# Decoding the expert choices one token block at a time, and preparing the last four expert slots first, in a decoder block on one core

## The chip, the cores and the metric

The kernel runs on one core of a Trainium2 chip. The metric is the device time of one execution in microseconds (us). The engines are named as in the profile: PE (TensorE: matrix products, with PEld its weight loads), DVE (VectorE), ACT (ScalarE), POOL (GpSimd) and SP (the queue that issues most of the DMAs). [...]

## The reference

One decoder block over 512 tokens of width 1024: an attention sub-layer (a sliding-window group and a stick-breaking group), a layer norm, then a sub-layer in which every token picks experts out of 16,384, and a second layer norm. The expert part, which the change touches, is this:

```python
q  = einsum('bsd,dk->bsk', xm, w_q).reshape(b, s, 8, 2, 128)
sc = einsum('bshpc,hpnc->bshpn', q, sub_keys)            # 8 heads, 2 halves, 128 keys
top_s, top_i = top_k(sc, 16)
cand = top_s[..., 0, :, None] + top_s[..., 1, None, :]   # 16 x 16 pairs
best_s, best_c = top_k(cand, 16)
i1 = take_along_axis(top_i[..., 0, :], best_c // 16)     # which key of half 0
i2 = take_along_axis(top_i[..., 1, :], best_c % 16)      # which key of half 1
expert = i1 * 128 + i2
g = softmax(best_s)
y[token] = sum over its 128 experts of g * gelu(xm . u[expert]) * v[expert]
```

All in float32 at the interfaces; the kernel holds most matrix operands as a high and a low part.

## The kernel before

**The expert part as matrix products.** The tokens are four blocks of 128. For blocks 1 to 3 (384 tokens) the kernel doesn't gather: it goes through all 128 slots of 128 experts. A U slot is 24 matmuls of 384 columns into `ph` (three for each of 8 chunks: `uhi` with `h2hi`, `uhi` with `h2lo`, `ulo` with `h2hi`), then Gelu into `stash`; a V slot is 18 matmuls of 512 columns into `yb`, with the weighted stash (`ghi`, `glo`) against the slot's rows of v (`vhi`, `vlo`). The weights are a table W of 384 tokens by 16,384 experts, built on chip from one-hot rows (`pw`) and written to `w_d`. Block 0 gathers its own experts' rows on POOL's DMA queue, and DVE works on them.

**High and low parts.** `split` (L91) makes `hi` with a copy on ACT and `lo` with a subtraction of 128x1024 on DVE or, where `eng=G`, on POOL. Two buffers each for `uhi` and `ulo`, so that the next slot's `uhi` starts when the slot two before it is done on PE. The third matmul of a slot needs `ulo`.

**The gate stage.** While DVE picks the top 16 (`top16`, L618 to L622, `cand` L632), PE runs U slots as cover. The last four of these (`MIDDLE`, recorded at L137) come directly before the choices are decoded, with their low parts on POOL. The last of them is called slot M here, and the one after it, the first of `u_steps`, slot N; N's `ulo` is made on DVE (the `split` in `cut`). From there on the order of instructions is the order of the code, on each engine. `decode` turns the 16 positions of every token and head into key positions `sel`, and the scores into weights `gall` (subtract, Exp on ACT, sum, reciprocal, multiply), on all four blocks at once (512 columns). `level2` of a block looks up `i1` and `i2` with one-hot compares of 128x2048 (`oh` L715, times `tabx` L717, folded L721), transposes (`ptr` L737) and makes the rows `tr` (L744, L745). Block 1's `level2` comes before the loop, interleaved with quarters of U slots (6 matmuls each) on PE.

**The W loop.** 96 groups of four tokens: `build` and `scale` (L758, L766, 128x1024) on DVE three groups ahead, 8 matmuls `pw` and about one quarter of a U slot on PE, and a share of the `level2` of the next block on DVE.

**The last stretch.** U slots run 32 ahead of V slots (`LOOK`), so the last V slots stand alone. `prep` makes a slot's operands: `gt` (L920), `glo` (L956), the v row's low part (L958); `heads` makes the high parts on ACT. `ghi` has three buffers and `glo` two; the last six slots (`GROUP`) take `glast` from the freed stash ring, and the last four put their v rows into the space of `h2hi` and `h2lo`, which U slots used before. `vraw` has three buffers, loaded by SP. The last six slots run as a group for each block and half of the columns, so that each token block is finished (`finish`: gate, add, layer norm, out) while PE works for the next.

## Time and profile before

| what | value |
|---|---|
| time, median of 3 runs | 1597.37 us (1597.34 to 1597.96) |
| the profiled execution: time, span | 1595.99 us, 1594.3 us |
| mean granted clock of PE in it | 0.985 |
| PE, DVE, ACT, POOL busy | 98%, 77%, 41%, 29% |
| PE's share of the chain that ended last | 79% |

The span is from the first to the last instruction; 1.7 us of the execution's time lie outside it. A busy PE is one with a matmul under way, at whatever clock.

### The profile page before, as it was taken

What the parts mean: (1) busy time and instruction counts of PE and PEld (TensorE: products, weight loads), DVE (VectorE), ACT (ScalarE), POOL (GpSimd) and SP (SyncE); (2) the same over time, 40 slices, a digit from 0 to 9 for tenths busy, and PEclk for the clock granted to TensorE, in tenths of its full rate; (3) what the DMA queues carried; (4) which work ended last, traced back from release to release, by engine and by line L of the source; (5) the groups of instructions that cost most, each with busy time, mean ns of one, the idle gap of its engine ahead of it and who ended that gap; (6) DMA issues with size and microseconds to landing.
All of it is one profiled execution on the core that took longest, in us unless ns stands there. A gap on an engine that the chain in (4) does not pass through costs nothing.

```text
span 1594.3 us, 21985 instructions
## 1 busy us (share of the span) xinstructions
PE 1554.9 (98%) x8109; PEld 1346.3 (84%) x8109; DVE 1220.3 (77%) x2351; ACT 647.5 (41%) x935; POOL 455.8 (29%) x410
## 2 busy tenths in 40 slices
PE   8999999999989999999999999999999999999996
PEld 5776767788879999899999999999999999998885
DVE  2568585589999997578777787777877777777878
ACT  2535574333355555333333333333333333333331
POOL 0002133544400000233334333333333444333100
PEclk8999898999999999999999999999999999999999
DMA  9564132222225555999888988999889998989873
GB/s 338 184 258 158 53 112 101 79 92 81 81 80 212 219 210 202 334 327 326 305 311 301 326 301 304 306 309 322 302 303 312 307 321 301 311 282 305 261 231 119
DMA packets 147356, 382.12 MB, mean 240 GB/s; under 512 B 11312, under 2 KB 68656, under 8 KB 143280
## 3 DMA queue, kind: packets, MB, share of 16 engines
q1 hardware_dynamic: 110384, 246.49, 44.6%
q0 software_dynamic: 36864, 134.23, 24.4%
q8 instruction: 63, 1.03, 0.3%
q14 instruction: 45, 0.37, 0.1%
HBM read 351.32 MB, written 29.36 MB: 239 GB/s over the span
## 4 chain that ended last, share of the span: by engine, by line
PE 79%; DVE 12%; DMA 3%; ACT 3%; issue 1%; POOL 1%; SPq 0%; DVEq 0%; ACTq 0%; POOLq 0%
PE yb L980 32%; PE ph L970 25%; PE pw L841 5%; PE ph L806 4%; PE pj L303 3%; PE zm L556 2%; DVE scr L620 1%; PE pj L274 1%; DMA wa<-in_wada_dram 1%; DVE tsi L622 1%; DVE tsi L619 1%; PE pq L647 1%; DVE tsv L621 1%; DVE tsv L618 1%; PE oacc L398 1%
## 5 line engine op out<-in xcount | busy, mean ns | idle before, releaser
L855 POOL DMA_INDIRECT gat<-in_u_rows_dram,idx x128 | 161.6, 1262 | 478.5 <-DVE hd L873 226.5
L93 DVE TENSOR_TENSOR ulo<-uraw,uhi 128x1024 fp32r<-128x1024 f32 x133 | 162.5, 1223 | 164.9 <-ACT uhi L92 160.5
L970 PE MATMUL ph<-h2hi,ulo 128*128 128x384 f32 x768 | 258.6, 337 | 0.6 <-DVE ulo L93 0.6
L970 PE MATMUL ph<-h2hi,uhi 128*128 128x384 f32 x768 | 258.2, 336 | 0.3 <-ACT uhi L92 0.3
L970 PE MATMUL ph<-h2lo,uhi 128*128 128x384 f32 x768 | 258.2, 336 | 0.0
L855 POOL DMA_INDIRECT gat<-in_v_rows_dram,idx x128 | 161.0, 1258 | 264.8 <-DVE y L883 224.1
L980 PE MATMUL yb<-vhi,ghi 128*128 128x512 f32 x654 | 203.0, 391 | 0.0
L980 PE MATMUL yb<-vhi,glo 128*128 128x512 f32 x654 | 202.9, 391 | 0.0
L980 PE MATMUL yb<-vlo,ghi 128*128 128x512 f32 x654 | 202.6, 391 | 0.0
L92 ACT ACTIVATE uhi<-uraw 128x1024 fp32r<-128x1024 f32 x155 | 162.4, 1050 | 74.6 <-PE pq L647 52.9
L883 DVE SCALAR_TENSOR_TENSOR y<-gat,cf,y 128x1024 f32<-128x1024 f32 x127 | 162.7, 1281 | 3.9 <-DMA gat<-in_v_rows_dram,idx 1.6
L873 DVE CUSTOM_DVE_ANT_0 gscr<-gat,h2row 128x1024 f32<-128x1024 f32 x128 | 156.5, 1222 | 10.6 <-DMA gat<-in_u_rows_dram,idx 7.9
L1085 ACT ACTIVATE stash<-ph 128x384 f32<-128x384 f32 x96 | 47.2, 491 | 275.1 <-PE ph L970 275.1
L970 PEld LDWEIGHTS ph<-h2lo,uhi 128*128 128x128 f32 x768 | 144.4, 188 | 4.4
L970 PEld LDWEIGHTS ph<-h2hi,uhi 128*128 128x128 f32 x768 | 144.4, 188 | 4.4 <-ACT uhi L92 0.7
L980 PEld LDWEIGHTS yb<-vlo,ghi 128*128 128x128 f32 x654 | 122.7, 188 | 27.3
L980 PEld LDWEIGHTS yb<-vhi,glo 128*128 128x128 f32 x654 | 122.8, 188 | 26.8
L970 PEld LDWEIGHTS ph<-h2hi,ulo 128*128 128x128 f32 x768 | 144.4, 188 | 1.0 <-DVE ulo L93 1.0
L980 PEld LDWEIGHTS yb<-vhi,ghi 128*128 128x128 f32 x654 | 121.8, 188 | 18.9
L93 DVE TENSOR_TENSOR vlo<-vraw,vhi 128x1024 fp32r<-128x1024 f32 x97 | 118.4, 1220 | 17.5 <-ACT vhi L92 17.4
L92 ACT ACTIVATE vhi<-vraw 128x1024 fp32r<-128x1024 f32 x97 | 102.8, 1060 | 53.6 <-issue 35.8
L947 ACT ACTIVATE ghi<-gt 128x384 fp32r<-128x384 f32 x97 | 51.0, 525 | 177.7 <-DVE gt L920 177.7
(311 smaller groups left out, 2860.1 us busy)
## 6 DMA issues: line engine op xcount, KB each, us to landing
uraw<-in_uT_dram SPq DMA_DIRECT2D x128, 512.0 KB, 5.2
vraw<-in_v_rows_dram SPq DMA_DIRECT2D x128, 512.0 KB, 5.2
w_d<-stage SPq DMA_DIRECT2D x12, 2048.0 KB, 7.3
wt<-w_d SPq DMA_DIRECT2D x32, 768.0 KB, 9.3
wa<-in_wada_dram SPq DMA_DIRECT2D x16, 1024.0 KB, 6.5
wah<-in_wada_dram SPq DMA_DIRECT2D x16, 512.0 KB, 9.4
uraw<-in_wq_dram SPq DMA_DIRECT2D x16, 512.0 KB, 3.3
uraw<-in_wqk_dram SPq DMA_DIRECT2D x11, 512.0 KB, 7.8
```

Source lines behind the costliest of these rows:

```text
L92: A.activation(hi, src, AF.Copy)
L93: (eng or V).tensor_tensor(lo, src, hi.bitcast(F32), op=OP.subtract)
L303: T.matmul(p, a[:, dc], b[:, dc], start=(dc == 0 and n == 0), stop=(dc == DC - 1 and n == 2))
L806: T.matmul(p[:, :ND], a[:, dc], b[:, dc, P:], start=(dc == 0 and n == 0), stop=(dc == DC - 1 and n == 2))
L841: T.matmul(p[:, k * P:(k + 1) * P], oh4[:, 1, :, k], oh4[:, 2 + j, :, k], start=(j == 0), stop=(j == 1), skip_group_check=True)
L855: G.indirect_dma_start(out=t, out_offset=None, in_=rows, in_offset=bass.IndirectOffsetOnAxis(ap=idx[:, k:k + 1], axis=0))
L873: V.tensor_tensor_reduce(out=scr, in0=t, in1=h2row, scale=1.0, scalar=0.0, op0=OP.mult, op1=OP.add, accum_out=hd[:, n:n + 1])
L883: V.scalar_tensor_tensor(y0, t, cf[:, k:k + 1], y0, op0=OP.mult, op1=OP.add)
L947: A.activation(gop[i][0], gts[i], AF.Copy)
L970: T.matmul(p[:, :ND], a[:, dc], b[:, dc, P:], start=(dc == 0 and n == 0), stop=(dc == DC - 1 and n == 2))
L980: T.matmul(ybank[b][c0 // 512][:, c0 % 512:(c1 - 1) % 512 + 1], x[:, t], y[:, c0:c1], start=(i == 0 and n == 0), stop=(n == 2 and i == (NK ...
L1085: A.activation(stash[i + LOOK], p[:, :ND], AF.Gelu_apprx_tanh)
```

## The change

In the gate stage the decoding is cut by token block. `weights` now comes first: the subtraction and the Exp for all four blocks, and the copy of the key indices. `decode(t0, t1)` then does block 1 alone (128 columns); blocks 2 and 3 (256 columns) and block 0 (128 columns) are decoded inside the W loop, ahead of the `level2` that needs them, at 19 steps a block where there were 15. Fewer steps stand before the loop, so that 12 quarters of U slots come before its first `pw` where there were 15, and three more inside it. Slot M's low part goes from POOL to DVE, and slot N's from DVE to POOL.

In the last stretch the last 14 slots (`OWN`) take `glast` for their weighted stash, where the last six did. The order of slots is now `seq`: 0 to 121, then 124 to 127, then 122 and 123. From slot 114 on operands are prepared four slots ahead and more, where it was two. `finish` of block 0 takes two steps a slot.

```diff
 GROUP = 6
+OWN = 14
 PRE = 0
...
 
-    def decode():
-        n = TB * P
-        pos = flat(bsp)
-        tmp = mw.tile([P, 4, n], BF16, name="dec", tag="oh", bufs=1)
+    def weights():
+        V.tensor_tensor(gall, bsv, bsv[:, :, :, 0:1].to_broadcast([P, TB, NH, TOPK]), op=OP.subtract)
+        A.activation(gall, gall, AF.Exp)
+        A.activation(tib, tsi, AF.Copy)
+
+    def decode(t0, t1):
+        c = slice(t0 * P, t1 * P)
+        pos = flat(bsp)[:, c]
+        tmp = mw.tile([P, 4, TB * P], BF16, name="dec", tag="oh", bufs=1)[:, :, c]
         pf, m1, m2, mk = (tmp[:, k] for k in range(4))
         d = pf
-        mi = mw.tile([P, n], U32, name="mi", tag="tabx", bufs=1)
-        A.activation(tib, tsi, AF.Copy)
+        mi = mw.tile([P, TB * P], U32, name="mi", tag="tabx", bufs=1)[:, c]
+        s0, s1 = sel[:, 0, c], sel[:, 1, c]
         V.tensor_copy(pf, pos)
-        yield
         V.tensor_scalar(m1, pf, 16.0, None, op0=OP.is_ge)
...
         V.tensor_tensor(mi, pos, mi, op=OP.bitwise_and)
-        yield
-        V.tensor_copy(sel[:, 1], mi)
-        V.tensor_tensor(d, pf, sel[:, 1], op=OP.subtract)
+        V.tensor_copy(s1, mi)
+        V.tensor_tensor(d, pf, s1, op=OP.subtract)
         yield
...
         V.tensor_tensor(d, d, mk, op=OP.mult)
-        yield
         V.tensor_tensor(d, d, m1, op=OP.subtract)
-        V.scalar_tensor_tensor(sel[:, 0], m2, -63.0, d, op0=OP.mult, op1=OP.add)
-        yield
-        V.tensor_tensor(gall, bsv, bsv[:, :, :, 0:1].to_broadcast([P, TB, NH, TOPK]), op=OP.subtract)
-        A.activation(gall, gall, AF.Exp)
+        V.scalar_tensor_tensor(s0, m2, -63.0, d, op0=OP.mult, op1=OP.add)
         yield
-        V.tensor_reduce(gsum[:, :, :, 0], gall, axis=AX.X, op=OP.add)
-        V.reciprocal(gsum, gsum)
-        V.tensor_tensor(gall, gall, gsum.to_broadcast([P, TB, NH, TOPK]), op=OP.mult)
+        g, q = gall[:, t0:t1], gsum[:, t0:t1]
+        V.tensor_reduce(q[:, :, :, 0], g, axis=AX.X, op=OP.add)
+        V.reciprocal(q, q)
+        V.tensor_tensor(g, g, q.to_broadcast([P, t1 - t0, NH, TOPK]), op=OP.mult)
         yield
...
 
-        def cut(s):
+        def cut(s, eng=V):
             if s < n1:
                 hl[s] = [wsp.tile([P, DC, P], F32R, name=f"u{e}", tag=f"u{e}") for e in ("hi", "lo")]
-                split(raws.pop(s), *hl[s])
+                split(raws.pop(s), *hl[s], eng)
 
...
         load(n0 + 1)
-        cut(n0)
+        cut(n0, G)
         yield
...
 
-    def slot_now():
-        u_slot(len(stash), bank("h", "ph", bufs=2), ring.tile([P, ND], F32, name="stash"))
-
-    for _ in range(MIDDLE):
-        slot_now()
+    for n in range(MIDDLE):
+        u_slot(len(stash), bank("h", "ph", bufs=2), ring.tile([P, ND], F32, name="stash"),
+               V if n == MIDDLE - 1 else G)
     man = tc.manual_schedule()
...
     next(us)
-    for n, _ in enumerate(chain(decode(), level2(1))):
+    weights()
+    for n, _ in enumerate(chain(decode(1, 2), level2(1))):
         if 2 * n >= 3 * done:
...
         if i % per == 0:
-            lv, ln = level2((2 + i // per) % TB), 0
+            tb = (2 + i // per) % TB
+            todo = () if tb == 3 else decode(tb, 4 if tb == 2 else 1)
+            lv, ln = chain(todo, level2(tb)), 0
         build(i + AHEAD)
...
         evac(i - 1)
-        while ln < 15 * (i % per + 1) / (per - AHEAD - 1):
+        while ln < 19 * (i % per + 1) / (per - AHEAD - 1):
             next(lv, None)
...
     vseen = set()
+    seq = list(range(NK - GROUP)) + list(range(NK - 4, NK)) + list(range(NK - GROUP, NK - 4))
 
-    def load_v(i):
-        if i < NK and i not in vseen:
+    def load_v(n):
+        i = seq[min(n, NK - 1)]
+        if n < NK and i not in vseen:
             vseen.add(i)
...
     def load_w(c):
-        if c < NK // WR:
+        if c < NK // WR and c not in wts:
             w = mw.tile([P, NTG, WR, TG], F32, name="wt")
...
         gts[i] = g.rearrange("p a t -> p (a t)")
-        gop[i] = [mw.tile([P, ND], F32R, name=f"g{e}", tag=f"g{e}", bufs=k) for e, k in (("hi", 3), ("lo", 2))]             if i < NK - GROUP else [
+        gop[i] = [mw.tile([P, ND], F32R, name=f"g{e}", tag=f"g{e}", bufs=k) for e, k in (("hi", 3), ("lo", 2))]             if i < NK - OWN else [
             ring.tile([P, ND], F32R, name="glast", tag="stash") for _ in range(2)]
...
 
-    def prep(i, units):
+    def prep(n, units):
         units = list(units)
+        i = seq[n] if n < NK else n
         alone = i + LOOK > NK
         if alone:
-            heads(i)
-            heads(i + 1)
+            for k in (n, n + 1):
+                if k < NK:
+                    load_w(seq[k] // WR)
+                    heads(seq[k])
         elif i < NK:
...
                 split(vraw.pop(i), *vop[i])
-        fetch_to(i + (LEAD if i + LOOK >= NK else 1))
+        fetch_to(n + (LEAD if n + LOOK >= NK else 1))
         for n in units:
...
                          start=(i == 0 and n == 0),
-                         stop=(n == 2 and i == (NK - GROUP - 1 if b == TB - 2 else NK - 1)) or c1 - c0 < 512,
+                         stop=(n == 2 and i == (NK - GROUP - 1 if b == TB - 2 else seq[-1])) or c1 - c0 < 512,
                          skip_group_check=(c1 - c0 < 512))
...
             return i + 1
-        return min(i + 2, NK - GROUP - 1) if i < NK - GROUP - 3 else min(NK, 2 * i - (NK - GROUP) + 8)
+        if i < NK - OWN:
+            return i + 2
+        return min(i + 4 + 3 * max(0, i - (NK - GROUP - 5)), NK)
 
...
             next(f0, None)
+            next(f0, None)
         if i == NK - GROUP - 1:
...
         for c in pieces(b + 1):
-            for i in range(NK - GROUP, NK):
+            for i in seq[NK - GROUP:]:
                 v_mm(i, b, (c,))
```

Three places in the order of DVE's instructions follow. The first is the end of the last head's `best`, where the decoding starts; `scr`, `bsv` and `bsp` are of the top 16, `ulo` is a U slot's low part. Before:

```order
L620 MATCH_REPLACE scr_3699<-bsv,cand 128x80
L621 MAX bsv<-scr_3699 128x8
L622 MAX_INDEX bsp<-bsv,scr_3699 128x8
L93 TENSOR_TENSOR ulo<-uraw,uhi 128x1024
L680 CAST dec<-bsp 128x512
L682 TENSOR_SCALAR dec<-dec 128x512
L683 TENSOR_SCALAR dec<-dec 128x512
L684 TENSOR_SCALAR dec<-dec 128x512
L686 SCALAR_TENSOR_TENSOR mi<-dec 128x512
```

After:

```order
L621 MATCH_REPLACE scr_3699<-bsv,cand 128x80
L94 TENSOR_TENSOR ulo<-uraw,uhi 128x1024
L622 MAX bsv<-scr_3699 128x8
L623 MAX_INDEX bsp<-bsv,scr_3699 128x8
L674 TENSOR_TENSOR gall<-bsv 128x512
L686 CAST dec<-bsp 128x128
L687 TENSOR_SCALAR dec<-dec 128x128
L688 TENSOR_SCALAR dec<-dec 128x128
L689 TENSOR_SCALAR dec<-dec 128x128
L691 SCALAR_TENSOR_TENSOR mi<-dec 128x128
```

The `ulo` ahead of the last MAX is slot M's; before, M's was POOL's, and the `ulo` that stood behind the last MAX_INDEX was slot N's. The subtraction of `gall` now stands ahead of the decoding, which is 128 wide.

The second place is the start of the W loop, where `oh_N` numbered rows are the one-hot rows for successive groups (L758 build, L766 scale). Before:

```order
L758 TENSOR_TENSOR oh_4025<-iota_2417,tr 128x1024
L758 TENSOR_TENSOR oh_4027<-iota_2417,tr 128x1024
L766 TENSOR_TENSOR oh_4025<-oh_4025,tr 128x1024
L758 TENSOR_TENSOR oh_4030<-iota_2417,tr 128x1024
L766 TENSOR_TENSOR oh_4027<-oh_4027,tr 128x1024
L758 TENSOR_TENSOR oh_4033<-iota_2417,tr 128x1024
L766 TENSOR_TENSOR oh_4030<-oh_4030,tr 128x1024
L715 TENSOR_TENSOR oh<-iota_2415,sel 128x2048
L758 TENSOR_TENSOR oh_4057<-iota_2417,tr 128x1024
L766 TENSOR_TENSOR oh_4033<-oh_4033,tr 128x1024
```

After:

```order
L759 TENSOR_TENSOR oh_4003<-iota_2417,tr 128x1024
L767 TENSOR_TENSOR oh_4000<-oh_4000,tr 128x1024
L759 TENSOR_TENSOR oh_4006<-iota_2417,tr 128x1024
L767 TENSOR_TENSOR oh_4003<-oh_4003,tr 128x1024
L686 CAST dec<-bsp 128x256
L687 TENSOR_SCALAR dec<-dec 128x256
L688 TENSOR_SCALAR dec<-dec 128x256
L689 TENSOR_SCALAR dec<-dec 128x256
L759 TENSOR_TENSOR oh_4033<-iota_2417,tr 128x1024
L767 TENSOR_TENSOR oh_4006<-oh_4006,tr 128x1024
L94 TENSOR_TENSOR ulo<-uraw,uhi 128x1024
L691 SCALAR_TENSOR_TENSOR mi<-dec 128x256
```

A quarter of the decoding of blocks 2 and 3 stands between two builds, where before it was the first compare of the next block's lookup, and the next part follows behind the `ulo`.

The third place is the last operands on DVE; `h2lo` is the low part of the v row of slots 124 to 127, `vlo` and `ulo` that of others. Before:

```order
L958 TENSOR_TENSOR h2lo<-vraw,h2hi 128x1024
L1038 SCALAR_TENSOR_TENSOR y_2423<-y_2423,l2rs,ln_13770 128x512 x2
L920 TENSOR_TENSOR gt<-stash,wt 128x384
L956 TENSOR_TENSOR glast<-gt,glast 128x384
L958 TENSOR_TENSOR h2lo<-vraw,h2hi 128x1024
L920 TENSOR_TENSOR gt<-stash,wt 128x384
L956 TENSOR_TENSOR glast<-gt,glast 128x384
L958 TENSOR_TENSOR h2lo<-vraw,h2hi 128x1024
L956 TENSOR_TENSOR glast<-gt,glast 128x384
L958 TENSOR_TENSOR h2lo<-vraw,h2hi 128x1024
```

After:

```order
L965 TENSOR_TENSOR h2lo<-vraw,h2hi 128x1024
L924 TENSOR_TENSOR gt<-stash,wt 128x384
L963 TENSOR_TENSOR glast<-gt,glast 128x384
L965 TENSOR_TENSOR h2lo<-vraw,h2hi 128x1024
L924 TENSOR_TENSOR gt<-stash,wt 128x384
L963 TENSOR_TENSOR glast<-gt,glast 128x384
L965 TENSOR_TENSOR h2lo<-vraw,h2hi 128x1024
L924 TENSOR_TENSOR gt<-stash,wt 128x384
L963 TENSOR_TENSOR glast<-gt,glast 128x384
L965 TENSOR_TENSOR vlo<-vraw,vhi 128x1024
L963 TENSOR_TENSOR glast<-gt,glast 128x384
L965 TENSOR_TENSOR ulo<-vraw,uhi 128x1024
```

The operands in the space of `h2lo` now come ahead of two that go to ordinary buffers (slots 122 and 123), and the last part of block 0's `finish` (L1038) is no longer between them.

## Rows read from the trace of the kernel before

**Rows 1.** The page: the span, two engines, and the lines of the chain
```profile
span 1594.3 us, 21985 instructions
...
PE 1554.9 (98%) x8109; PEld 1346.3 (84%) x8109; DVE 1220.3 (77%) x2351; ACT 647.5 (41%) x935; POOL 455.8 (29%) x410
...
PE yb L980 32%; PE ph L970 25%; PE pw L841 5%; PE ph L806 4%; PE pj L303 3%; PE zm L556 2%; DVE scr L620 1%; PE pj L274 1%; DMA wa<-in_wada_dram 1%; DVE tsi L622 1%; DVE tsi L619 1%; PE pq L647 1%; DVE tsv L621 1%; DVE tsv L618 1%; PE oacc L398 1%
```

**Rows 2.** Windows: busy us by engine, granted clock (PEclk), DMA share, GB/s
```profile
437.80:461.00 23.20, 18.52 (x88) 17.40 (x87) 20.27 (x34) 12.46 (x15) 0.00 (x0) 0.85 0.28 91
...
452.00:454.00 2.00, 2.00 (x8) 2.00 (x7) 1.86 (x5) 1.97 (x2) 0.00 (x0) 0.50 0.64 234
...
480.00:500.00 20.00, 20.00 (x145) 18.29 (x144) 20.00 (x33) 10.70 (x16) 0.00 (x0) 1.00 0.64 232
...
655.00:1443.00 788.00, 788.00 (x3993) 717.07 (x3992) 608.82 (x749) 286.48 (x382) 305.87 (x241) 1.00 0.90 311
```

**Rows 3.** Timeline of PE, 427 to 475 us
```profile
432.50 0.34 PE L137 MATMUL ph<-h2hi,ulo 128*128 128x384 f32 x1
...
445.41 0.34 PE L806 MATMUL ph<-h2hi,ulo 128*128 128x384 f32 x1
...
449.60 0.69 PE L806 MATMUL ph<-h2hi,uhi 128*128 128x384 f32 x1 [3.85 <-ACT uhi L92]
...
456.14 0.44 PE L806 MATMUL ph<-h2hi,uhi 128*128 128x384 f32 x1
...
462.67 1.11 PE L841 MATMUL pw<-oh 128*128 128x128 f16 x8 [0.95 <-DVE oh L766]
...
472.10 1.11 PE L841 MATMUL pw<-oh 128*128 128x128 f16 x8 [0.27 <-DVE oh L766]
```

**Rows 4.** Timeline of DVE, 428 to 463 us
```profile
429.16 2.48 DVE L632 TENSOR_TENSOR cand<-tsv 128x16 f32<-128x16 f32 x2
...
435.45 0.23 DVE L620 MATCH_REPLACE8 scr<-bsv,cand 128x80 f32<-128x80 f32 x1
...
436.22 1.21 DVE L93 TENSOR_TENSOR ulo<-uraw,uhi 128x1024 fp32r<-128x1024 f32 x1
...
437.35 0.42 DVE L680 CAST dec<-bsp 128x512 bf16<-128x512 uint32 x1
...
445.03 0.69 DVE L701 TENSOR_REDUCE gsum<-gall 128x32 f32<-128x512 f32 x1 [0.70 <-ACT gall L699]
...
446.75 1.22 DVE L715 TENSOR_TENSOR oh<-iota,sel 128x2048 bf16<-128x2048 bf16 x1
...
449.57 1.23 DVE L93 TENSOR_TENSOR ulo<-uraw,uhi 128x1024 fp32r<-128x1024 f32 x1 [1.61 <-ACT uhi L92]
...
460.52 0.29 DVE L745 TENSOR_TENSOR tr<-gr,tr 128x128 f16<-128x128 f32 x1
...
461.93 0.68 DVE L766 TENSOR_TENSOR oh<-oh,tr 128x1024 f16<-128x1024 f16 x1
```

**Rows 5.** Line L632 by engine: least, median and longest in ns
```profile
L632 DVE TENSOR_TENSOR cand<-tsv x7: 156/178/2403, 428.8 to 432.1; 128x32 f32<-128x32 f32 x2, 128x20 f32<-128x20 f32 x1, 128x16 f32<-128x16 f32 x1, 128x12 f32<-128x12 f32 x1
```

**Rows 6.** Timelines of POOL and ACT, 427 to 449 us
```profile
429.21 2.40 POOL L93 TENSOR_TENSOR ulo<-uraw,uhi 128x1024 fp32r<-128x1024 f32 x1 [1.74 <-ACT uhi L92]
...
432.23 1.06 ACT L92 ACTIVATE uhi<-uraw 128x1024 fp32r<-128x1024 f32 x1 [2.72 <-PE ph L137]
...
446.70 1.90 ACT L709 ACTIVATE tabx<-tib 128x2048 bf16<-128x2048 bf16 x1
```

**Rows 7.** Waits of PE, 1443 to 1595 us
```profile
PE yb L980 <- DVE h2lo L958: 3.1, 3, 1.2
```

**Rows 8.** Timelines of PE and DVE in the last stretch
```profile
1559.03 0.50 PE L980 MATMUL yb<-h2lo,glast 128*128 128x512 f32 x1 [1.21 <-DVE h2lo L958]
...
1561.60 1.22 DVE L958 TENSOR_TENSOR h2lo<-vraw,h2hi 128x1024 fp32r<-128x1024 f32 x1
```

**Rows 9.** Waits of DVE, 1443 to 1565 us
```profile
DVE glo L956 <- PE yb L980: 21.1, 23, 2.5
```

## The prediction before the run

> **What bounds the kernel now.** First the page: PE is busy 98% of 1594.3 us, and four of its lines make up 66% of the chain that ended last [rows 1]. From 655 to 1443 us it has no pause at all: 788.00 busy us of 788.00, at full clock, for 95 U and 95 V slots, so 4.15 us a slot and 1.04 us for a quarter of a U slot; a V slot has 18 matmuls, 0.23 us each [rows 2]. The loop of W is full too (20.00 of 20.00 for PE and for DVE between 480 and 500 us [rows 2]). Whatever shifts PE's work before such a stretch passes through it unchanged. Only pauses of PE, its clock, and work added to it count, so I read its waits, stage by stage.
>
> In the gate stage, 437.8 to 461 us, PE is busy 18.52 of 23.20 us while DVE has 20.27 and the granted clock is 0.85 [rows 2]. [...] The first `pw` starts at 462.67 after a wait for DVE's `oh`, and there is another short wait in the loop at 472.10 [rows 3].
>
> In the last stretch PE waits three times for `h2lo`, 3.1 us together [rows 7], from 1559.03 on [rows 8]. Counted from start to start at 0.23 us a matmul, PE loses 3.6 us there. DVE was not short of time over the stretch as a whole: it waited 21.1 us for `glo` buffers that PE still read [rows 9].
>
> The sums go by the profiled execution, 1595.99 us; the median is 1.4 above it, and I add the change to the median, 1597.4.
>
> **The last stretch.** With `glast` for 14 slots, the wait of [rows 9] is gone for these, and DVE prepares four slots ahead where it had two. A slot costs DVE one 1.22 us subtraction [rows 8], in the steady case starting its successor 1.14 later as at 436.22 and 437.35 [rows 4], and two on 384 columns (about 0.5 each, worked out from the 0.69 of 512 columns [rows 4]): 2.2 us. Two slots done earlier take 4.4 us from the end; the last `lo` ended at 1562.8 [rows 8] and would end near 1558.4. PE needs it with the last group's 17th matmul, 0.23 x 16 after the group's start; that start is 1559.03 less the 1.4 that this wait costs and 10 matmuls, so 1555.3, and the need falls at 1559.0. The margin is 0.6 us. Putting 124 to 127 first costs nothing: their space has been free since the last U slot, so their operands wait for no buffer. The loads of `vraw` keep three buffers, and could hold the chain for a slot; then one pause of about 1.5 us stays. **Term: -3.6**, bounds -2.1 and -4.0.
>
> **The gate stage, slot M.** PE reaches M's third matmul at 432.50 [rows 3] and then needs its low part. On POOL it started at 429.21 [rows 6]. On DVE it stands behind the last MATCH_REPLACE, at 435.45 before [rows 4]. But DVE was itself held up: its additions for `cand` at 429.16 took 2.48 us for two [rows 4], the longest 2.403 us where the least is 0.156 [rows 5], just while POOL's subtraction of 2.40 us ran from 429.21 [rows 6]. With that subtraction gone from POOL, 2.24 us come back, and DVE reaches M's low part at 433.2 + 0.15 = 433.4. POOL now has N's instead: its `uhi` runs from 432.23 for 1.06 us, so POOL can start at 433.3 to 433.4 [rows 6]. The two starts fall together, and each wants what the other would hold.
>
> - *DVE first.* M's low part ends at 434.6; PE stalls 2.1 us (432.50 to 434.6). POOL runs until 437.0, and the subtraction of `gall` is held until then.
> - *POOL first.* DVE is held until 435.8, M's low part ends at 436.95, PE stalls 4.4 us. That is longer than the 3.85 us after which the clock fell [rows 3].
>
> [...] If the two only ran side by side, `gall` would start 2.1 us sooner and the sum below would be 1591.0. [...]
>
> **To the first `pw`.** Before, the first compare (L715) stood at 446.75 and `pw` at 462.67 [rows 3, 4], 15.9 us with three `ulo` of 1.14 and a pause of 1.6 at 449.57 for a `uhi` that came late behind the Exp [rows 4]. After, one `ulo` is ahead of the compare and Exp is early, so 15.9 - 1.14 - 1.6 = 13.2. The 512-wide decoding took from 437.35 to 446.75 less one `ulo` and the 0.70 of waiting for Exp at 445.03 [rows 4], 7.6 us, of which 0.6 is `gall`. At 128 columns a row like that at 460.52 is 0.29 where one of 512 columns is 0.69 [rows 4], so 7.0 x 0.42 = 2.9, with 0.2 for gaps 3.1. With DVE first the compare is then at 437.0 + 0.6 (`gall`) + 3.1 + 1.1 (`ulo`) = 441.8 and its multiply due at 443.0, but `tabx` takes 1.90 us on ACT [rows 6] and comes behind the `uhi` that M's end at 438.2 releases and the return to Gelu, by 444.0 or so. So 1.0 more, and the first `pw` is at 441.8 + 1.0 + 13.2 = 456.0. PE has then done 12 quarters, not 15; three of 1.04 to 1.15 are owed in the loop, 3.3 us. 456.0 + 3.3 = 459.3 against 462.67: **-3.4**, bounds -3.0 and -3.8.
>
> **The W loop.** Blocks 2 and 3 (256 columns, 14 instructions) now stand in the first eight groups, block 0's later. Between 128 and 512 columns the durations lie on a line, so a 256-wide row is about 0.42 and the decoding 4.4 us; bounds half and all of the 512-wide one, 3.5 and 7.0. A build and a scale are 1.2 us together (0.68 each, 0.60 apart [rows 4]) against PE's 1.9 to 2.0 a group; that slack of 0.7 to 0.8 also has to hold the lookup and a `ulo`, and was just used up (the wait of 0.27 at 472.10 [rows 3], and DVE 20.00 of 20.00 [rows 2]). Laying the new order's rows one behind the other, PE waits 1.5 us at its sixth group and 1.4 at its eleventh, 2.9, less the 0.27 of before. **Term: +2.7**, bounds +1.7 and +5.2. It costs nothing only if the builds ran more than three groups ahead, and they don't.
>
> **Sum, DVE first:** -3.6 - 3.4 + 2.7 = -4.3, so 1593.1 us; own range 1591.5 to 1597.5 by the bounds.
>
> **The rivals.**
>
> - *POOL first, and the clock falls.* PE's stall of 4.4 us also delays M's end, the next `uhi`, and the `ulo` that DVE's order puts ahead of its sums: the first `pw` comes 1.7 us later, at 457.7, and a fall as before adds 3.3: 461.0, plus 3.3 owed, 464.3 against 462.67, +1.6. In all -3.6 + 1.6 + 2.7 = +0.7: 1598.1, no change. For it: the start by 433.3 is POOL's by a hair, and the stall is longer than the one that halved the clock. Against: the hair.
> - *POOL first, clock stays.* -3.6 - 1.7 + 2.7 = -2.6: 1594.8. PE ran without a pause before 432.50, which it also did before 445.41, so this is the weaker half.
> - *DVE first, but 2.1 us are enough for the clock to fall.* It costs about 2.5, since part of the 3.3 lies under DVE's chain: 1595.6. Only 3.85 is known to do it.
> [...]
> - *The end doesn't move* because `vraw` loads hold it: then 1.5 to 3.6 us of the first term are missing and DVE first gives 1594.6 to 1596.7. It is within the first case's own range.
>
> **How the numbers follow.** DVE first 0.40; POOL first with the fall 0.34; POOL first without 0.11; DVE first with a fall 0.08; the long fall 0.07. The two orders are close to even, since the two starts agree within my error of some 0.2 us. The likeliest single case gives 1593.1. Faster than 1594.2 are four fifths of the first case (0.32), a third of the third (0.04), and 0.04 from the others: 0.40. Slower than 1600.6: 0.07, and a tenth of the second, 0.10 in all. The rest, 0.50, is the same. The range from 1591.5 to 1599.5 leaves out some 0.06 below and 0.13 above.
>
> **What would show it.** Right: the three waits for `h2lo` near 1560 gone; PE's wait at M's third matmul 2.1 us with POOL's N behind DVE's M, and no 0.50 clock near 440; the additions for `cand` near 429 short; the first `pw` near 456; two waits of about 1.5 us for `oh` in the first eleven groups. Wrong: POOL's N starting ahead of DVE's M with a PE pause over 4 us and a half clock behind it; waits for `oh` that add up to more than 5 us; or a wait for `vlo` or `ulo` of slots 122 and 123 in place of that for `h2lo`.

## The result and the profile after

The changed kernel takes 1605.04 us (median of 6 runs, 1604.44 to 1606.65) against 1596.59 us before: ratio 1.0055, interval 1.0043 to 1.0068. It is 8.4 us slower. The prediction had 1593.1, and a range that ends at 1599.5.

Of the page of the changed kernel: its span, the engines, and the lines of the chain (its line numbers are 1 to 7 higher than those of before).

```profile
span 1603.6 us, 22011 instructions
...
PE 1556.5 (97%) x8109; PEld 1345.3 (84%) x8109; DVE 1223.1 (76%) x2381; ACT 648.0 (40%) x935; POOL 455.7 (28%) x410
...
PE yb L987 31%; PE ph L977 25%; PE pw L843 5%; PE ph L807 5%; PE pj L304 3%; PE zm L557 2%; DVE scr L621 1%; PE pj L275 1%; DMA wa<-in_wada_dram 1%; DVE tsi L623 1%; DVE tsi L620 1%; DMA wt<-w_d 1%; PE pq L648 1%; DVE tsv L622 1%; DVE tsv L619 1%
```

PE has as many matmuls as in [rows 1] and is busy 1.6 us longer in a span 9.3 us longer. To find where, I put the two profiles side by side by stages, from the starts of PE's rows: the last `psc` (the scores' product, ahead of slot M), the first and the last `pw`, the first `yb`, the last `ph`, and the end.

| stage (us) | before | after | difference |
|---|---|---|---|
| start to last `psc` (untouched) | 420.22 | 418.52 | -1.70 |
| last `psc` to first `pw` (gate stage) | 42.45 | 37.73 | -4.72 |
| first to last `pw` (W loop) | 169.29 | 176.15 | +6.86 |
| last `pw` to first `yb` | 23.42 | 23.64 | +0.22 |
| first `yb` to last `ph` | 787.69 | 787.69 | 0.00 |
| last `ph` to the end (last stretch) | 151.23 | 159.87 | +8.64 |

The long middle repeats to 0.01 us. The gate stage and the loop together lose 2.1 us where -0.7 was forecast, and the last stretch loses 8.6 where -3.6 was forecast.

**The gate stage after.** PE's waits from 416 to 655 us, which answer to those behind [rows 3]:

```profile
PE pw L843 <- DVE oh L767: 3.2, 2, 2.0
...
PE ptr L738 <- DVE i L722: 2.5, 1, 2.5
...
PE ph L138 <- DVE ulo L94: 2.2, 2, 2.0
```

the wait for `oh` in the kernel before, of which 0.95 us stands ahead of the first `pw` and 0.7 in the loop:

```profile
PE pw L841 <- DVE oh L766: 1.6, 3, 0.9
```

and the four that matter in the changed kernel's PE timeline:

```profile
432.94 0.44 PE L138 MATMUL ph<-h2hi,ulo 128*128 128x384 f32 x1 [1.97 <-DVE ulo L94]
...
452.78 0.33 PE L738 MATMUL ptr<-ident,i 128*128 128x128 f32 x1 [2.48 <-DVE i L722]
...
456.25 1.11 PE L843 MATMUL pw<-oh 128*128 128x128 f16 x8 [1.98 <-DVE oh L767]
...
477.34 1.11 PE L843 MATMUL pw<-oh 128*128 128x128 f16 x8 [1.23 <-DVE oh L767]
```

The 3.85 us pause of [rows 3] is gone, and pauses at M's third matmul (1.97), ahead of the transposes (2.48), ahead of the first `pw` (1.98) and in the loop (1.23) have come. Windows of the changed kernel (the number behind POOL's is the granted clock as a share of full speed):

```profile
432.00:437.00 5.00, 4.06 (x15) 4.06 (x16) 4.83 (x12) 2.56 (x3) 3.12 (x1) 0.70 0.49 156
...
446.00:450.00 4.00, 4.00 (x24) 3.82 (x23) 3.83 (x5) 1.82 (x3) 0.00 (x0) 1.00 0.41 133
...
454.50:461.30 6.80, 5.04 (x26) 4.85 (x27) 6.76 (x14) 2.45 (x4) 0.00 (x0) 0.50 0.10 39
...
478.40:481.80 3.40, 3.40 (x18) 3.09 (x17) 3.40 (x8) 1.11 (x2) 0.00 (x0) 0.50 0.43 169
...
1562.00:1566.00 4.00, 2.02 (x5) 0.98 (x4) 2.83 (x5) 2.25 (x4) 0.00 (x0) 0.73 0.92 275
...
1566.00:1570.00 4.00, 2.23 (x4) 0.79 (x3) 2.20 (x3) 1.47 (x2) 0.00 (x0) 0.50 0.82 326
...
1570.00:1575.00 5.00, 4.43 (x12) 3.56 (x13) 2.59 (x4) 0.00 (x0) 0.00 (x0) 0.59 0.01 3
```

The clock is 0.70 behind the pause at M, 1.00 in between, 0.50 around the first `pw`, from 454.5 to 461.3 us, and again 0.50 for 3.4 us behind the pause in the loop. In the kernel before, the whole loop had 1.00:

```profile
462.70:632.00 169.30, 168.60 (x1205) 155.21 (x1205) 158.51 (x249) 88.60 (x141) 0.00 (x0) 1.00 0.52 193
```

The last three rows of the changed kernel are of the last stretch, and come back below.

**The start of M's and N's low parts.** On DVE (the first is M's `ulo`, the second the subtraction of `gall`) and on POOL (N's `ulo`):

```profile
431.67 1.22 DVE L94 TENSOR_TENSOR ulo<-uraw,uhi 128x1024 fp32r<-128x1024 f32 x1
...
433.30 2.37 DVE L674 TENSOR_TENSOR gall<-bsv 128x512 f32<-128x512 f32 x1
...
431.67 3.46 POOL L94 TENSOR_TENSOR ulo<-uraw,uhi 128x1024 fp32r<-128x1024 f32 x1 [5.90 <-ACT uhi L93]
```

Both start at 431.67. DVE's takes its usual 1.22 us and POOL's 3.46 where the like row in [rows 6] took 2.40, 1.06 us more. Then `gall`, 0.68 us in the kernel before, takes 2.37 under the rest of it. That is the order "DVE first" of the prediction, with starts that are the same to the 0.01 us that the trace shows.

**The last stretch after.** PE's waits from 1443 us on, which answer to [rows 7]:

```profile
PE yb L987 <- DVE h2lo L965: 2.9, 3, 1.2
...
PE yb L987 <- DVE ulo L965: 2.3, 2, 1.4
...
PE yb L987 <- ACT glast L941: 1.3, 2, 0.7
...
PE yb L987 <- DVE vlo L965: 0.9, 1, 0.9
```

7.4 us where there were 3.1. The waits for `h2lo`, which were to go, are nearly as long as before; beside them stand those that the prediction named as a sign of being wrong, for `vlo` of slot 122 and `ulo` of slot 123 (0.9 us each), and one of 1.4 for `ulo` of slot 121. DVE, over the same slots: its longest waits, and three rows of its timeline around them.

```profile
DVE gt L924 <- DMA wt<-w_d: 10.9, 2, 6.7
...
1529.10 1.22 DVE L965 TENSOR_TENSOR vlo<-vraw,vhi 128x1024 fp32r<-128x1024 f32 x1
...
1536.97 0.56 DVE L924 TENSOR_TENSOR gt<-stash,wt 128x384 f32<-128x384 f32 x1 [6.66 <-DMA wt<-w_d]
...
1551.60 0.56 DVE L924 TENSOR_TENSOR gt<-stash,wt 128x384 f32<-128x384 f32 x1 [4.22 <-DMA wt<-w_d]
```

DVE does what the change wants of it until 1530.3: the row at 1529.10 is slot 118's, between two and three slots ahead of PE. Then it stands 6.66 us, and 4.22 us further on, for the weights `wt` of slots 120 to 123 and 124 to 127. `heads` of the next slot puts the `gt` of slot 120 ahead of the low parts of slot 119, so these wait too. What SP did in that time:

```profile
1525.10 5.61 SPq L906 DMA_DIRECT2D vraw<-in_v_rows_dram  x3
...
1530.75 0.43 SPq L911 DMA_DIRECT2D wt<-w_d  x1
...
1543.86 0.33 SPq L906 DMA_DIRECT2D vraw<-in_v_rows_dram  x1
...
1544.24 0.43 SPq L911 DMA_DIRECT2D wt<-w_d  x1
```

The load of the weights is issued at 1530.75, when the three loads of V rows ahead of it in SP's queue are through. The last of them goes out just behind the end of DVE's row of 1529.10, which sets its buffer free. So the weights are asked for just when DVE wants them, and come 6.2 us later. At 1543.86 and 1544.24 the same happens again.

### The profile page after: what moved, and what is told of

The parts are those of the page before. It is cut to its first block, busy times and chain, and to the rows that moved or that the text cites. A ratio compares the mean times of both kernels' runs of the same rounds, so it can differ in the third digit from the quotient of the medians.

```text
span 1603.6 us, 22011 instructions
## 1 busy us (share of the span) xinstructions
PE 1556.5 (97%) x8109; PEld 1345.3 (84%) x8109; DVE 1223.1 (76%) x2381; ACT 648.0 (40%) x935; POOL 455.7 (28%) x410
## 4 chain that ended last, share of the span: by engine, by line
PE 78%; DVE 13%; DMA 4%; ACT 3%; issue 1%; POOL 1%; SPq 0%; DVEq 0%; ACTq 0%; POOLq 0%
PE yb L987 31%; PE ph L977 25%; PE pw L843 5%; PE ph L807 5%; PE pj L304 3%; PE zm L557 2%; DVE scr L621 1%; PE pj L275 1%; DMA wa<-in_wada_dram 1%; DVE tsi L623 1%; DVE tsi L620 1%; DMA wt<-w_d 1%; PE pq L648 1%; DVE tsv L622 1%; DVE tsv L619 1%
## 5 line engine op out<-in xcount | busy, mean ns | idle before, releaser
L987 PE MATMUL yb<-vhi,ghi 128*128 128x512 f32 x630 | 195.6, 391 | 0.0
L987 PE MATMUL yb<-vhi,glo 128*128 128x512 f32 x630 | 195.5, 391 | 0.0
L987 PE MATMUL yb<-vlo,ghi 128*128 128x512 f32 x630 | 195.2, 391 | 0.0
L987 PEld LDWEIGHTS yb<-vlo,ghi 128*128 128x128 f32 x630 | 118.2, 188 | 26.3
L987 PEld LDWEIGHTS yb<-vhi,glo 128*128 128x128 f32 x630 | 118.3, 188 | 25.8
L987 PEld LDWEIGHTS yb<-vhi,ghi 128*128 128x128 f32 x630 | 117.3, 188 | 17.9
```

The costliest lines, as they stand in the source:

```text
L987: T.matmul(ybank[b][c0 // 512][:, c0 % 512:(c1 - 1) % 512 + 1], x[:, t], y[:, c0:c1], start=(i == 0 and n == 0), stop=(n == 2 and i == (NK ...
```

## The experiments

All differences are against the kernel before on the same chip (1596.67, 1597.32 and 1597.75 us in the three groups of runs); in us they are worked out from the ratio, which can differ by up to 1 us from the difference of the two medians.

**The two halves apart.** `e1_gate_only` has the changed gate stage with the old last stretch, `e2_end_only` the reverse.

> Only the gate stage is changed; the last stretch is that of the kernel before. In the profiles of before and after, counted from the start of slot M's high part on ACT, the first V slot starts 2.4 us later in the changed kernel, and the stretch from there to the end is 8.6 us longer. If the two parts add up, this one is 2.4 us slower than before (1.0015), with PE pauses of about 2 us at M's third matmul and ahead of the first pw and half clock behind them. Rival: the gate stage in itself gains as forecast (-0.7), and the 2.4 us come from elsewhere between the two marks; then it is not slower than before.

> Only the last stretch is changed; the gate stage is that of the kernel before. Theory: all of the 8.6 us belongs to it, so 8 to 9 us slower than before (1.0054), with DVE idle for some 11 us in two waits for the weights wt behind the V loads on SP's queue. Rival: the last stretch suffers only because of what the gate stage leaves behind (other buffers, other timing); then under 4 us slower.

Measured: gate stage alone 1599.55 us, 1.0015 (1.0004 to 1.0026); last stretch alone 1603.15 us, 1.0041 (1.0025 to 1.0057). The halves add up to the whole within the intervals, 2.4 + 6.5 against 8.4, and the rivals fall, though 6.5 is also less than the 8 to 9 expected. In `e2_end_only` DVE waits 12.5 us for `wt` from 1500 us on. The loss is mostly the last stretch's own.

**The weights early, and the engines swapped back.** Both start from the changed kernel.

```diff
     for i in range(NK):
+        if i in (NK - 15, NK - 13):
+            load_w(i // WR + 2 + (i == NK - 13))
         load_u(i + LOOK + 2)
```

> The changed kernel, but the weights of slots 120 to 123 and 124 to 127 are loaded at the start of the steps of slots 113 and 115, ahead of the V loads that wait for DVE. Theory (weights late): DVE's two waits of 6.7 and 4.2 us go, it keeps its lead, and the last stretch is 1 to 4 us shorter than that of before: total within 2 us of before (0.998 to 1.001). Rival (the three buffers of the V rows hold the stretch, and the weights are only what happens to be waited for): waits for the V rows take their place and it stays over 5 us slower than before.

Measured: 1595.81 us, 0.9999 (0.9987 to 1.0011), some 9 us better than the changed kernel. Its SP timeline shows the two loads 10 to 13 us sooner than above:

```profile
1520.67 0.43 SPq L911 DMA_DIRECT2D wt<-w_d  x1
...
1531.58 0.43 SPq L911 DMA_DIRECT2D wt<-w_d  x1
```

From 1500 us on, no wait of DVE for `wt` is left, and with it the loss of the last stretch has gone; whether late weights lose as much by themselves, `e11_vgat_wt_late` shows below. But the last stretch is 151.9 us and not 1 to 4 us below the 151.2 of before, since something is left: PE's and ACT's waits of this kernel from 1443 and 1540 us on.

```profile
PE yb L987 <- DVE ulo L965: 1.2, 1, 1.2
...
PE yb L987 <- DVE vlo L965: 0.8, 1, 0.8
...
ACT h2hi L939 <- DMA vraw<-in_v_rows_dram: 3.6, 2, 2.1
```

ACT waits for the V rows, and PE for the slots at the end of the order, 122 and 123. The rival had a part of the truth.

```diff
-               V if n == MIDDLE - 1 else G)
+               G)
...
-        cut(n0, G)
+        cut(n0)
```

> The changed kernel, but slot M's low part stays on POOL and slot N's on DVE. Theory (the swap's pause and the half clock behind it): the PE pause of 2 us at M's third matmul goes, the clock stays at full there, and although the additions for cand are held up again for 2.2 us the first pw comes 1 to 3 us earlier, so 6 to 8 us slower than before. Rival (the decoding inside the loop is the cost): the first pw and the loop's waits stay as they are, 8 to 10 us slower than before, or more by the 2.2 us.

Measured: 1605.40 us, 1.0050 (1.0031 to 1.0069). The pause at M and the 0.70 behind it are gone as expected, but the first `pw` is 0.7 us later, not earlier (38.45 us from the last `psc`), and the loop as long (175.9). The theory falls, and the rival has it: stages and time stay nearly as they are. DVE's additions for `cand` are held up again (the longest takes 2.4 us), DVE waits 1.66 us for the `uhi` of the slot behind N all the same, and the pauses ahead of the transposes and of the first `pw` are still there (2.48 and 1.76 us). It seems that what PE lost at M it loses further on, where DVE sets the pace, but no run separates the two. The swap neither costs nor gains what a measurement here can tell.

**What holds the last stretch beside the weights.** `e6_end_vgat` is the changed last stretch with early weights, and three V rows in other buffers.

```diff
-            vraw[i] = mw.tile([P, D], F32, name="vraw", bufs=3)
+            vraw[i] = (mw.tile([P, D], F32, name="vgat", tag="gat", bufs=RING) if n in (NK - 5, NK - 3, NK - 1)
+                       else mw.tile([P, D], F32, name="vraw", bufs=3))
```

> The gate stage of before, the changed last stretch with the weights loaded early, and three of the last six V rows loaded into buffers of the gather ring that are free by then, so that the last rows have more than three buffers. Theory (with the weights in time, the loads of the V rows through three buffers are what still holds the stretch): PE's waits at the last slots, 2.3 us with the weights early, go, and the kernel is 2 to 4 us faster than before. Rival (DVE's work for block 0's finish between the slots holds it): under 1 us of difference to before.

Measured: 1591.21 us, 0.9966 (0.9953 to 0.9980), 5.4 us faster than before, more than the 2 to 4 expected, and all runs within 2.8 us. PE waits nowhere in the last stretch, which takes 147.5 us. Its windows, the last two rows, behind the same two of the kernel before:

```profile
1555.00:1560.00 5.00, 3.78 (x16) 2.41 (x14) 5.00 (x9) 2.72 (x5) 0.00 (x0) 1.00 0.88 286
...
1560.00:1565.00 5.00, 3.09 (x12) 2.27 (x13) 4.07 (x5) 1.09 (x2) 0.00 (x0) 1.00 0.80 318
...
1555.00:1560.00 5.00, 4.99 (x23) 3.77 (x22) 4.17 (x7) 0.65 (x2) 0.00 (x0) 1.00 0.42 151
...
1560.00:1565.00 5.00, 5.00 (x23) 4.11 (x22) 2.93 (x5) 0.00 (x0) 0.00 (x0) 1.00 0.02 5
```

To see which of the pieces does it, `e11_vgat_wt_late` leaves out the early weights, and `e12_before_vgat` puts the other buffers into the kernel before, without the change (the same edit, with `i` for `n`).

> The gate stage of before, the changed last stretch, with the three V rows in buffers of the gather ring but the weights loaded where the change has them. Theory (the late weights are the loss, by themselves; more V buffers then help little, since SP's queue holds the weights behind the V loads all the same): DVE's two waits for wt stay, 3 to 6 us slower than before. Rival (more V buffers unblock the queue, and the weights come in time): no wait for wt, and 3 us or more faster than before.

Measured: 1598.68 us, 1.0008 (0.9992 to 1.0023): no difference that can be told, and less of a loss than the 3 to 6 us expected, but DVE's wait is as it was:

```profile
DVE gt L924 <- DMA wt<-w_d: 10.7, 3, 6.4
```

So late weights alone are not the loss. With three buffers they make the last stretch 6.5 us slower than before (`e2_end_only`), with the other buffers 1.3 (-1.3 to 3.7), and PE's waits are 3.8 us in place of 6.4. The loss needs both, the late weights and the three buffers. Moving the weights brings 9 us with the three buffers, and 6.7 with the others (1.3 to -5.4).

> The kernel before with one edit: three of the last six V rows in buffers of the gather ring. Theory (DVE's lead, which the change of the last stretch brings, is needed beside the buffers): the three waits for h2lo shrink by a third at most, under 2 us faster. Rival (the V rows' loads are all that holds the end of before): the waits go, and it is 3 to 6 us faster, as much as with the changed and mended last stretch.

Measured: 1594.43 us, 0.9983 (0.9971 to 0.9995), 2.7 us faster (0.8 to 4.6), between the theory's under 2 and the rival's 3 to 6. PE's three waits for `h2lo` are still 2.6 us (3.1 in [rows 7]), as the theory had it; where the rest of the gain comes from isn't shown. By the runs, then, buffers alone bring half of the 5.4 us; the waits go only with DVE's lead, the weights in time and the buffers together. What the new order of slots and the 14 `glast` slots do each by itself was not tried.

**The kernel before once more**, for a second profile.

> The kernel before, unchanged, for a second profile of its stages. Every theory here counts stage by stage; if the stages repeat, the gate stage (last psc to first pw) takes 42.4 us, the loop 169.3 and the last stretch 151.2, each within 0.5 us. If the last stretch differs by some us, its waits hang on when the V rows land, and a difference of that size between kernels says nothing.

The gate stage is 42.48 us and the loop 169.4, both as expected, but the last stretch 153.8. Its windows, and PE's wait:

```profile
1555.00:1560.00 5.00, 2.29 (x7) 0.97 (x6) 4.81 (x7) 1.94 (x4) 0.00 (x0) 0.89 1.00 354
...
1560.00:1565.00 5.00, 4.75 (x11) 3.78 (x12) 2.27 (x4) 0.00 (x0) 0.00 (x0) 0.50 0.28 113
...
PE yb L980 <- DVE h2lo L958: 3.0, 3, 1.2
```

The wait is that of [rows 7] to 0.1 us, and yet the clock fell behind it, which it did not in the first profile. Five profiles with the old last stretch have 151.2, 153.8, 155.3, 155.4 and 154.3 us. So 151.2 was the shortest of them, and of the 8.6 us only some 5.9 are over the mean, 154.0. The last three of the five stand behind a changed gate stage; over the two of the kernel before the 8.6 would be 7.3. Both agree with the 6.5 (4.0 to 9.1) measured for that half.

**The gate stage.** Two kernels with the old last stretch and two with the mended one look for what is lost there. `e5_fill15` sets the quarters closer, with the old last stretch.

```diff
-        if 2 * n >= 3 * done:
+        if 5 * n >= 6 * done:
```

> The changed gate stage with the last stretch of before, and one edit: quarters of U slots are set 5 for every 6 steps of the decoding and lookup, so that 15 and not 12 stand ahead of the first pw, as before the change. In the changed kernel PE pauses 2.5 us ahead of the transposes and 2.0 ahead of the first pw and then runs at half clock. Theory (PE was left without work while DVE sets the pace): those pauses are filled, the first pw stays within 1 us of the changed kernel's, the three owed quarters (3.3 us) and the half clock behind the pauses (about 2) go; 1 to 4 us faster than before. Rival (the extra quarters bring their low part forward on DVE, and the first pw comes as much later): within 1 us of the gate stage alone, 2 to 3 us slower than before.

Measured: 1601.58 us, 1.0027 (1.0010 to 1.0044), 4.3 us slower than before: the theory falls, and neither expectation has the number. The first `pw` comes 3.3 us later than in the changed kernel (40.99 us from the last `psc`), and the loop takes 176.0 us although nothing is owed in it. But its profile shows another thing too, so that not all of this is the quarters' doing. POOL's and DVE's start of N's and M's low parts, and PE's matmul that waits for M's:

```profile
429.81 2.34 POOL L93 TENSOR_TENSOR ulo<-uraw,uhi 128x1024 fp32r<-128x1024 f32 x1 [5.89 <-ACT uhi L92]
...
429.89 3.33 DVE L93 TENSOR_TENSOR ulo<-uraw,uhi 128x1024 fp32r<-128x1024 f32 x1
...
433.28 0.69 PE L137 MATMUL ph<-h2hi,ulo 128*128 128x384 f32 x1 [4.17 <-DVE ulo L93]
```

Here POOL was 0.08 us ahead, DVE's subtraction took 3.33 us, and PE paused 4.17 us with 0.58 granted from 434 to 440: the prediction's second case, from the same order of instructions up to there. Where the kernel before shows DVE alone held up beside POOL (0.156 us at least, 2.403 in [rows 5]), these two traces show both directions: POOL's 2.40 us became 3.46 beside DVE's in the changed kernel, and DVE's 1.22 became 3.33 beside POOL's here. Which of the two a run gets isn't fixed by the program: of the six profiles with the swap, five have DVE first (POOL's row takes 3.41 to 3.46 us), with starts at most 0.05 us apart.

`e7_all_ahead` decodes all four blocks ahead of the loop.

```diff
-    for n, _ in enumerate(chain(decode(1, 2), level2(1))):
+    for n, _ in enumerate(chain(decode(0, 4), level2(1))):
...
-            todo = () if tb == 3 else decode(tb, 4 if tb == 2 else 1)
+            todo = ()
...
-        while ln < 19 * (i % per + 1) / (per - AHEAD - 1):
+        while ln < 15 * (i % per + 1) / (per - AHEAD - 1):
```

> The changed gate stage with the last stretch of before, but all four blocks are decoded ahead of the loop, in one go, and none in it: Exp first, the swap of engines and 12 quarters ahead of the loop are kept. Theory (the decoding inside the loop costs what it takes there, in waits and in the clock): the first pw comes 4 us later than with block 1 alone, and the loop from first to last pw is 3 to 5 us shorter than 176.1, so 2 to 4 us slower than before in all. Rival (the loop has room for it, and its length comes from the owed quarters and the clock alone): the loop stays at 175 to 176, and the whole is 5 to 7 us slower than before.

Measured: 1598.47 us, 1.0013 (1.0000 to 1.0027), as the theory had it in all. The first `pw` comes 2.1 us later (39.82), not 4, and the loop takes 172.7 us: 3.4 over before, with the three owed quarters in it. Without the decoding, the one wait for `pw` is that ahead of the first; but the clock was at half there too, into the loop:

```profile
PE pw L842 <- DVE oh L766: 1.1, 1, 1.1
...
457.90:460.90 3.00, 2.99 (x15) 2.68 (x15) 3.00 (x5) 2.66 (x3) 0.00 (x0) 0.50 0.00 0
```

`e10_noswap_fill15` has the whole change with the mended last stretch, M and N on their old engines, and 15 quarters ahead; `e9_gate_fixed_end` has the whole change with the mended last stretch only (edits as above).

> The whole change with both mends of the last stretch (weights early, three V rows in buffers of the gather ring). With this end the executions spread by under 3 us, so the gate stage can be read cleanly against the same end on the gate stage of before (0.9966). If the parts add up as the stages of the profiles say (the gate stage and the loop 2.1 us longer), 0.9979, some 3.4 us faster than before; if the gate stage is no loss, 0.9966.

Measured: 1592.17 us, 0.9970 (0.9958 to 0.9981), 4.8 us faster than before. It lies between the two expectations, and the interval holds both: beside the 5.4 us of `e6_end_vgat` no loss of the gate stage can be told, though by stages it is there (213.85 us from last `psc` to last `pw`, where the kernel before has 211.74). PE waits nowhere in the last stretch, which takes 147.2 us. The change with both mends is thus faster than before.

> The whole change with the mended last stretch, slot M's low part kept on POOL and slot N's on DVE, and 15 quarters of U slots ahead of the first pw. Theory (the gate stage loses by PE's pauses and the half clock behind them, and by the three owed quarters, not by the decoding in the loop): no pause at M, the pauses ahead of the first pw filled; last psc to last pw 207 to 210 us where it was 211.8, so 0.9940 to 0.9960. Rival (DVE sets the pace: each quarter ahead brings a low part that delays the first pw as much): 212 to 215 us, 0.997 to 0.999.

Measured: 1592.41 us, 0.9971 (0.9958 to 0.9984), and 213.3 us from last `psc` to last `pw`: the rival's numbers. But not by its mechanism, for the first `pw` is no later than with 12 quarters (38.42, and 38.45 in `e4_no_swap`). The loop takes 174.9 us although nothing is owed in it, because PE now waits five times for `oh`, once for 1.24 us ahead of the first `pw` and for 3.8 us in the loop, and the clock falls there once:

```profile
PE pw L843 <- DVE oh L767: 5.0, 5, 1.4
...
468.10:471.50 3.40, 3.40 (x20) 3.09 (x19) 3.33 (x8) 1.22 (x3) 0.00 (x0) 0.50 0.00 1
```

So owed quarters alone make the loop 3.4 us longer (`e7_all_ahead`), the decoding alone 5.6 (`e10_noswap_fill15`), and both 6.9. A part of each is the clock: half of the 3.0, 3.4 and 8.4 us that PE worked at 0.50 in the loop, 1.5, 1.7 and 4.2 us. Without it 1.9, 3.9 and 2.7 us are left. They don't add: where DVE sets the pace, quarters in the loop fill PE's waits, which are 3.8 us for `oh` without owed quarters and 1.2 with them.

## Why the prediction was wrong

**The last stretch: the step that failed.** "-3.6, bounds -2.1 and -4.0" came out as +6.5 by the runs of that half, and +8.6 in the one profile. The prediction followed three of a slot's inputs to DVE (the stash buffer, the V rows, the space of `h2lo`) and not the fourth, the weights. It was right that DVE has the time, that the wait of [rows 9] goes for the 14 slots (13.7 us are left of 21.1 in the same stretch, all ahead of them), and that the lead is real until 1530. It took it that a lead of four slots can be kept, and did not ask what each load needs to be four slots early. `wt` has its place in SP's queue by PE's slot number, as before, behind V loads that now follow DVE. `e3_wt_early` shows it: with two lines that move these loads, 9 us come back. The loss takes the three buffers of the V rows as well: with more of them and the weights as late, 1.3 us of the 6.5 are left (`e11_vgat_wt_late`).

The sentence on `vraw` ("could hold the chain for a slot; then one pause of about 1.5 us stays") was right as a mechanism: with the weights early, 2.3 us of waits are left, and with more buffers none. With the weights early alone, the whole is 0.2 us faster than before and the gate half 2.4 slower, so the last stretch gains some 2.6 us, inside the bounds; each interval is some 2 us to either side. With both mends it gains 5.4, but 2.7 of these the buffers, which are no part of the change, bring to the kernel before by themselves. That 147.5 us against the 151.2 of the first profile gives the forecast's size is luck: against the second profile of the same kernel, 153.8, it would be 6.3.

The clock, for which the term had nothing, made it worse. In the profile PE's waits grew by 4.3 us. Behind them PE ran with 0.73, 0.50 and 0.59 granted (the windows from 1562 to 1575): 2.02 x 0.27 + 2.23 x 0.50 + 4.43 x 0.41 = 3.5 us of work lost. That is 7.8 of the 8.6.

**To the first `pw`: -6.7 forecast, -4.7 measured.** The order (DVE first), the pause at M (1.97; forecast 2.1), the short additions for `cand` (0.21 us at most) and the end of `gall` were right. The step that failed is that 2.1 us are too short for the clock to fall, an estimate from the 3.85 us of [rows 3] alone. Behind the 1.97 us it fell at once (0.70 from 432 to 437 us); M ended later, the next `uhi` started at 438.52 where 436.5 would follow from the forecast, and DVE stood 1.23 us for it, the larger part of the 1.95 us that were missing. The rival that said so had 0.08. This is read from one trace; `e4_no_swap`, where the pause and the fall at M are gone, can't confirm it, since it gives back the 2.2 us of `cand`.

**The W loop: +6.0 forecast (3.3 owed and 2.7), +6.9 measured.** The size is nearly right, but by luck. PE's waits for `oh` in the loop were 1.23 us, one and not two of 1.5, 0.5 over the 0.7 of before. The larger part is the clock, for which the sum had nothing: 5.0 and 3.4 us of PE's work in the loop at 0.50, where before had 1.00 throughout, cost 4.2 us. That leaves 2.1 us for the three owed quarters, reckoned at 3.3. In the prediction's own sum of bounds there is a slip as well: -4.0 - 3.8 + 1.7 is -6.1, so its own range begins at 1591.3, not 1591.5.

**The rivals.** By the number the nearest is the long fall (0.07), half clock from 437 us to the first `pw`, with 1604, and that is luck: the clock was 1.00 again from 446 to 450 us, and the loss lies in the last stretch, where this rival too had -3.6. For the gate stage and the loop, "DVE first, but 2.1 us are enough for the clock to fall" was right in mechanism and in size: its -3.4 + 2.5 + 2.7 = +1.8 stands against +2.1 by stages and +2.4 in `e1_gate_only`. "POOL first, and the clock falls" was seen once, in `e5_fill15`. The 3.3 us that the rivals count for a fall as before are half of the 6.5 us from 449.60 to 456.14 in the kernel before [rows 3], where the clock was 0.50 [rows 2]. None had the last stretch lose more than its gain. The "end doesn't move" rival stopped at zero; a bound below zero needed only the question what DVE would wait for next.

## What to carry to other kernels

When operands are prepared further ahead, list every input of the operand and find, for each, where its load stands in the issuing queue and what the loads ahead of it wait for; here the load of `wt` kept its old place and became the next wait, 6.66 and 4.22 us of DVE's time. A term for "work done ahead" has a loss as its far bound until each of these is shown to be early enough. In a stretch that begins behind a pause, look at the clock as well: in this loop it was 4.2 of the 6.9 us. And where two waits in one stretch have different causes (a bound engine, owed work), try one without the other before adding them up.

## What was unexpected

- In these profiles the clock didn't follow from the length of a pause alone. In the gate stage and the loop it was 0.50 behind a pause of 3.85 us in the kernel before, 0.70 from 432 to 437 us around one of 1.97 and 0.50 behind one of 1.23 in the changed kernel, and it stayed at 1.00 behind one of 0.95 in the kernel before and one of 1.24 in `e10_noswap_fill15`. Near 612 us a pause of 1.34 us in `e5_fill15` was followed by a fall and one of 1.36 us in `e10_noswap_fill15`, at the same place of the program, by none (0.79 granted from 612 to 620 us, against 1.00 from 611.6 to 620). The three waits at the end of the kernel before, 3.1 and 3.0 us, left the clock at 1.00 in one profile and took it to 0.50 in the other.
- Run to run, over three chips, the kernel before spreads from 1589.8 to 1602.1 us. Part of it is ahead of the change: the last `psc` starts between 416.7 and 420.2 us in fourteen profiles, by the same instructions. Part is the last stretch: `e6_end_vgat`, with no wait there and the old gate stage, spreads by 2.8 us only; the same last stretch with the changed gate stage (`e9_gate_fixed_end`) spreads by 6.6, and what that comes from wasn't followed up.
- The first `yb` to the last `ph`, 787.69 us, was equal in all profiles to 0.01 us, with the DMA queues 90% busy [rows 2].
